# Modulation folds moved out of the key/value stage, and tile-wise hand-over of banks, in a one-core diffusion step

## The chip, the cores and the metric

The kernel runs on one NeuronCore of a Trainium2 chip. Its engines are TensorE (PE: matmuls; PEld: its weight loads), VectorE (DVE), ScalarE (ACT), GpSimd (POOL) and SyncE (SP), which issues most DMAs; each runs its own instructions in order and waits for the others through semaphores. The metric is the device time of one execution in microseconds, the median of several runs. Lnnn is a line of the kernel before; in the changed kernel the same statement has a number that is two or three higher.

## The reference

One layer of a hybrid diffusion backbone over 1024 latent tokens and 128 context tokens (1152 in all, 9 tiles of 128), model width 1024, float32:

```
m  = silu(c) @ w_ada + b_ada            # six vectors per condition ("modulation")
h  = rmsnorm(x) * (1 + scale) + shift
[u | q | k | v | gates] = h @ w_in      # 512 | 1024 | 256 | 256 | 2048 columns
f  = real(fft2(u))                      # 4 groups of 128 channels
a  = windowed attention(q, rope(k), v)  # 16 heads, 4 kv heads of 64, window 128, sink logit
x1 = x + g1 * (merge(f @ w_fo, a @ w_ao, sigmoid(gates)) @ w_out)
y  = x1 + g2 * (relu(h2 @ w1)**2 @ w2)  # h2: x1 normed and modulated
```

Latent queries read a window of latent keys and 128 cached context keys in one softmax; context queries read context keys alone. Keys and values of the context are outputs too. The modulation is computed for two condition vectors. The attention, norms and the rest of the modulation need only parts of m at a time.

## The kernel before

**Precision and weights.** A float32 matrix is split into a high part and a remainder ("whi" and "wlo", by `split`: an ACT cast at L144, a DVE subtraction at L139), and a product takes three matmuls (L192 to L194, L230 to L232). Weights come as "wraw" by SP's queue (L153).

**Stages in the profiled execution.** 0 to 174 us: norm, Fourier projection, gates, DFT. 174 to 302 us, the KV stage: `tok_proj_round` projects keys and values for the token tiles in ROUNDS, 6 tiles in round 0 and 3 in round 1, eight blocks k of the contraction each; between the rounds stand the six query pieces of head group 0. Each tile has one PSUM bank "x" of pool qk, which `evac_kv` empties (values: L691; keys: rope on DVE, or L708 for the context tile; the context outputs go through "ra" and "rb" at L711). 302 to 747 us, attention. Then the Fourier branch's output, the gate and attention-output stage from 800 us, and the output projection and MLP.

**Attention.** 36 units, one for each head group g and query block i. A unit has four score heads (`score_head`: two matmuls L755 and L756 into "s", a masked minimum on DVE L757, exp on ACT L767, and after each pair of heads the scaling on POOL L779), then for every key block a transpose group `out_t` (L789 into "ptp", the cast "ph" L792 on ACT and the remainder "pl" on DVE) and a value product `out_v` (L804 and L805 into the single bank "o"; after the last one the copy "ot" L813 and the addition "at" L814 empty it). Keys are transposed by `put_k` (L835, cast "kth" L837). TensorE's order in the KV stage and in attention is written out by hand (`manual_schedule`); the other engines' orders come from a scheduler. `unit_order` lists a unit's steps with None at each spot where fill may go: the fill steps are query pieces of the next group, gate pieces and parts of the Fourier output (L926, L947). `NSPR` sets how many are spread over the units; the rest stays for the end. The value product of block 0 stands right behind the third out_t of its own unit; the others stand between the score heads of the next unit (`late`).

**Modulation.** The remaining four vectors are computed in 16 blocks of 256 columns by ten steps each (`mod_blocks`). Steps 0 to 7 load a piece "mraw" of w_ada (L303), multiply it by a number per partition for two conditions on ACT (L307, into "macc" in step 0, into the one "mprod" buffer after that), and add on POOL (L309). In later stages both are one DVE operation (L316). Steps 8 and 9 transpose and reduce on DVE (L325, L326) into "red". `mod_fold` sums over partitions with a matmul of 16 columns (L272), and DVE adds the bias into "mods". A fold is issued at step 5 of the next block. Before each k of a KV round some steps are issued (50 in the two rounds), in attention one after each pair of heads (60 in all), ten behind attention, and 40 later. Two gate vectors are written to the scratch tensor ga_d and read back broadcast (L1106).

**Pools.** A tile pool that reuses the memory of an earlier, closed pool starts, without further words, only when all work on the earlier one is done. With reuse_waits="tile" each tile waits for the users of its own piece alone.

## Time and profile before

| | us |
|---|---|
| median of 3 runs (lowest, highest) | 1721.02 (1719.16, 1723.3) |
| the profiled execution's own time | 1719.39 |
| its span | 1717.6 |
| TensorE busy | 1621.3 |
| DVE, ACT, POOL busy | 1133.9, 909.4, 279.1 |
| KV stage to the first key transpose | 174.4 to 302.6 |
| attention | 302.6 to 747 |

The span is what the trace covers; the own time is 1.8 us longer. A row of a timeline gives start, duration, engine and line, the operation with output <- inputs, its shape, and in brackets how long the engine had stood idle before and who released it. Matmuls are pipelined: the distance of two starts, not the duration, is what one costs. The row of a window gives its length, then each engine's busy time and instructions, TensorE's granted clock (1.00 is full), the DMA engines' busy share and GB/s.

### The profile page before, as it was taken

The page shows a single profiled execution, that of the slowest core. Times are in us where ns is not written, and L with a number is a line of the kernel's source. Part 1 is how long each engine was busy: PE and PEld are TensorE (multiplying, and loading weights), DVE is VectorE, ACT ScalarE, POOL GpSimd, SP SyncE. Part 2 cuts the span into 40 slices and gives each one's busy share as a digit, 9 for nine tenths or more (in the row PEclk, how much of TensorE's full clock was granted, in tenths as well). Part 3 has the DMA queues.
Part 4 walks back from the last instruction along what each step waited for, and adds up shares of the span by engine and source line. Part 5 has one row for each costly group of instructions (what it writes and reads, how often), then busy time and mean ns, then how long its engine had stood idle before and what let it go on. Part 6 is the DMA issues. An engine that isn't in the chain of part 4 may idle for free.

```text
span 1717.6 us, 24946 instructions
## 1 busy us (share of the span) xinstructions
PE 1621.3 (94%) x8421; PEld 1426.9 (83%) x8421; DVE 1133.9 (66%) x2164; ACT 909.4 (53%) x1759; POOL 279.1 (16%) x375
## 2 busy tenths in 40 slices
PE   6999396999999999999999989999999999999998
PEld 5799385898998989979988788888888888888887
DVE  6563056576676776777557877777775588777764
ACT  7733344567577666646336574444444354444542
POOL 1010353334344443310001400000000200000000
PEclk9999698999999999999999999999999999999999
DMA  8441356943445342269545425445446896656751
GB/s 296 132 142 68 118 159 167 187 131 101 108 126 152 100 117 74 87 205 299 173 171 194 166 99 174 154 163 168 162 160 156 264 392 230 190 186 196 243 173 62
DMA packets 221136, 285.41 MB, mean 166 GB/s; under 512 B 30968, under 2 KB 148664, under 8 KB 220880
## 3 DMA queue, kind: packets, MB, share of 16 engines
q1 hardware_dynamic: 212752, 273.85, 50.4%
q0 software_dynamic: 8256, 9.96, 2.5%
q8 instruction: 66, 1.08, 0.3%
q14 instruction: 62, 0.51, 0.1%
HBM read 205.87 MB, written 77.88 MB: 165 GB/s over the span
## 4 chain that ended last, share of the span: by engine, by line
PE 70%; DVE 5%; DMA 3%; ACT 3%; issue 2%; POOL 1%; SPq 1%; DVEq 0%; ACTq 0%; POOLq 0%
PE x L1845 6%; PE x L1843 6%; PE x L1844 6%; PE x L1447 6%; PE x L1449 6%; PE x L1448 6%; PE mm L192 4%; PE mm L194 4%; PE mm L193 4%; PE ptp L789 2%; PE x L194 2%; PE x L193 2%; PE x L192 2%; PE s L756 2%; PE o L805 2%
## 5 line engine op out<-in xcount | busy, mean ns | idle before, releaser
L139 DVE TENSOR_TENSOR wlo<-wraw,whi 128x1024 fp32r<-128x1024 f32 x109 | 139.9, 1285 | 99.4 <-ACT whi L144 98.8
L144 ACT CAST whi<-wraw 128x1024 fp32r<-128x1024 f32 x107 | 111.8, 1049 | 88.2 <-DMA wraw<-in_w_in_dram 22.5
L193 PE MATMUL mm<-BR,whi 128*128 128x384 f32 x408 | 137.9, 338 | 0.0
L767 ACT ACTIVATE pt<-pt,mx 128x513 f32<-128x513 f32 (+2 forms) x144 | 95.9, 666 | 75.6 <-DVE mx L757 72.4
L1844 PE MATMUL x<-BR 128*128 128x512 f32 (+1 forms) x348 | 132.8, 382 | 0.0
L192 PE MATMUL mm<-BR,whi 128*128 128x384 f32 x360 | 129.4, 360 | 3.0 <-DVE qt L633 2.1
L1845 PE MATMUL x<-BR 128*128 128x512 f32 (+1 forms) x348 | 132.2, 382 | 0.0
L1843 PE MATMUL x<-BR 128*128 128x512 f32 (+1 forms) x348 | 131.3, 382 | 0.0
L779 POOL TENSOR_SCALAR pt<-pt,mx 128x512 f32<-128x512 f32 (+2 forms) x144 | 95.9, 679 | 212.9 <-DVE mx L777 212.6
L757 DVE CUSTOM_DVE_ANT_0 pt<-s,mask,nsink 128x512 f32<-128x512 f32 (+2 forms) x144 | 96.4, 671 | 41.4 <-PE s L756 40.2
L194 PE MATMUL mm<-BR,wlo 128*128 128x384 f32 x360 | 122.3, 340 | 0.0
L309 POOL TENSOR_TENSOR macc<-macc,mprod 128x512 f32<-128x512 f32 x77 | 102.1, 1326 | 42.9 <-ACT mprod L307 32.8
L139 DVE TENSOR_TENSOR pl<-ptp,ph 128x512 fp32r<-128x512 f32 x124 | 82.9, 686 | 38.2 <-ACT ph L792 37.6
L1816 ACT CAST BR<-aa 128x512 fp32r<-128x512 f32 x80 | 49.7, 621 | 101.7 <-PE x L1844 46.3
L307 ACT ACTIVATE mprod<-mraw,siluc 128x256 f32<-128x256 f32 x154 | 70.2, 502 | 46.8 <-POOL macc L309 45.8
L1447 PE MATMUL x<-BR,whi 128*128 128x512 f32 (+2 forms) x204 | 79.4, 389 | 4.1 <-ACT ZR L1471 2.8
L193 PEld LDWEIGHTS mm<-BR,whi 128*128 128x128 f32 x408 | 77.9, 191 | 6.3
L792 ACT CAST ph<-ptp 128x512 fp32r<-128x512 f32 x124 | 69.9, 583 | 20.3 <-PE ptp L789 18.7
L1449 PE MATMUL x<-BR,wlo 128*128 128x512 f32 (+2 forms) x204 | 77.9, 382 | 0.0
L1448 PE MATMUL x<-BR,whi 128*128 128x512 f32 (+2 forms) x204 | 77.6, 380 | 0.0
L192 PE MATMUL mm<-BT,whi 128*128 128x384 f32 x216 | 76.5, 354 | 0.0
L1844 PEld LDWEIGHTS x<-BR 128*128 128x128 f32 x348 | 65.4, 188 | 12.9
(450 smaller groups left out, 4733.6 us busy)
## 6 DMA issues: line engine op xcount, KB each, us to landing
aa<-hr_d SPq DMA_DIRECT2D x108, 256.0 KB
ab<-in_w_ff_dram SPq DMA_DIRECT2D x108, 256.0 KB
hr_d<-ZR SPq DMA_DIRECT2D x104, 256.0 KB
wraw<-in_w_in_dram SPq DMA_DIRECT2D x41, 512.0 KB
wraw<-in_w_ff_dram SPq DMA_DIRECT2D x34, 512.0 KB
mraw<-in_w_ada_dram SPq DMA_DIRECT2D x96, 128.0 KB
wraw<-in_w_out_dram SPq DMA_DIRECT2D x24, 512.0 KB
z_d<-z SPq DMA_DIRECT2D x48, 192.0 KB
```

Of the source, the lines that this page charges most:

```text
L139: eng.tensor_tensor(dst, raw, hi.bitcast(F32), ALU.subtract)
L144: nc.scalar.copy(hi, raw)
L192: nc.tensor.matmul(out, ah, bh, start=start, stop=False)
L193: nc.tensor.matmul(out, ah, bl, start=False, stop=False)
L194: return nc.tensor.matmul(out, al, bh, start=False, stop=stop).ins
L309: nc.gpsimd.tensor_tensor(acc, acc, pr_, ALU.add)
L1447: nc.tensor.matmul(po, wh, xh, start=(k == 0 and not cont), stop=False, skip_group_check=cont)
L1448: nc.tensor.matmul(po, wh, xl, start=False, stop=False, skip_group_check=cont)
L1449: nc.tensor.matmul(po, wl, xh, start=False, stop=(k == 3), skip_group_check=cont)
L1843: nc.tensor.matmul(ps, xh, bh, start=start, stop=False, skip_group_check=cont)
L1844: nc.tensor.matmul(ps, xh, bl, start=False, stop=False, skip_group_check=cont)
L1845: nc.tensor.matmul(ps, xl, bh, start=False, stop=stop, skip_group_check=cont)
```

## The change

- **Folds.** From the KV rounds to the end of attention no fold is issued at step 5. Instead, after each unit from the fourth on, one block is folded, as long as one younger one is there. "red" has 8 buffers in place of 2.
- **Modulation steps.** 30 before the KV rounds' blocks k (round 0 alone: 4 each, 2 before the last), none in round 1; in attention from the second unit on, two steps after the first pair of heads and one after the second, until 60 are left (70 steps over 24 units); 20 behind attention, and 40 later as before.
- **Hand-over.** Pools pq, q1 and q3 wait by tile. The two query buffers "qT" lie in two pools, pq and p1.
- **Value products.** All of a unit's products stand between the score heads of the next unit; ph and pl have 4 buffers in place of 3.
- **Tail.** 11 fill steps in place of 6 are kept for the end, one after each of the last value products.
- **Other.** Two "fo" buffers in place of one; dynamic_dma_scratch_size=4096, by which more SBUF is free and the small pool pk (rope, ra, qr) lies in memory of its own, so that SP's queue has the loads of rope and of the cached keys and values among the first ones.

```diff
-MOD_A = (1, 1)
+MOD_A = (2, 1)
-MOD_B = 50
+MOD_B = 60
...
-    def mod_fold():
+    fold_auto = [True]
+
+    def mod_fold(keep=0, most=99):
         nb = MB // P
-        while fold:
+        for _ in range(min(most, len(fold) - keep)):
             blk, red = fold.pop(0)
...
-                    if k == 5:
+                    if k == 5 and fold_auto[0]:
                         mod_fold()
...
-                        st["r"] = const.tile([P, 2, MB // 32], F32, tag="red", name=nm("red"), bufs=2)
+                        st["r"] = const.tile([P, 2, MB // 32], F32, tag="red", name=nm("red"), bufs=8)
...
-            tok_proj_round(ROUNDS[0], OFF_KV, bankk, evac_kv, before=lambda k: mod_step(4))
+            fold_auto[0] = False
+            tok_proj_round(ROUNDS[0], OFF_KV, bankk, evac_kv, before=lambda k: mod_step(4 if k < 7 else 2))
             for piece in q_pieces(0):
...
-            tok_proj_round(ROUNDS[1], OFF_KV, bankk, evac_kv, before=lambda k: mod_step(2 if k < 7 else 4))
-        pq = s1x.enter_context(tc.tile_pool(name="pq", bufs=1))
-        q1 = s1x.enter_context(tc.tile_pool(name="q1", bufs=1, space=PSUM))
+            tok_proj_round(ROUNDS[1], OFF_KV, bankk, evac_kv)
+        pq = s1x.enter_context(tc.tile_pool(name="pq", bufs=1, reuse_waits="tile"))
+        q1 = s1x.enter_context(tc.tile_pool(name="q1", bufs=1, space=PSUM, reuse_waits="tile"))
...
-            qt = pq.tile([P, 4, CH], F32R, tag="qT", name=nm("qT"), bufs=2)
+            qt = (pq if (g * NJ + j) % 2 else p1).tile([P, 4, CH], F32R, tag="qT", name=nm("qT"), bufs=1)
...
-            if len(msteps) > MOD_B:
+            if len(msteps) > MOD_B and u["s"]:
                 with tc.issue_after(ins.ins):
                     mod_step(min(MOD_A[pr], len(msteps) - MOD_B))
...
-            ph = p1.tile([P, 512], F32R, tag="ph", name=nm("ph"), bufs=3)
-            pl = p1.tile([P, 512], F32R, tag="pl", name=nm("pl"), bufs=3)
+            ph = p1.tile([P, 512], F32R, tag="ph", name=nm("ph"), bufs=4)
+            pl = p1.tile([P, 512], F32R, tag="pl", name=nm("pl"), bufs=4)
...
             for b in range(nb):
                 out += [lambda b=b: out_t(prev, b), None]
-                if b == 2:
-                    out += [None, lambda: out_v(prev, 0), None]
-            if 0 < nb < 3:
-                out += [None, lambda: out_v(prev, 0), None]
-            late += [(prev, b) for b in range(1, nb)]
+            late += [(prev, b) for b in range(nb)]
             return out
...
-        NSPR = NSUB - 16 - 6
+        NSPR = NSUB - 16 - 11
...
             pending = u
+            if s > 2:
+                mod_fold(1, 1)
+        out_t(pending, 0)
         for v in late:
+            fill_to(base + 1)
             out_v(*v)
-            fill_to(base + 1)
-        out_t(pending, 0)
+            base += 1
         fill_to(NSUB)
...
         man.close()
+        fold_auto[0] = True
         mod_step(len(msteps) - MOD_B)
         mod_fold()
 
-    q3 = ctx.enter_context(tc.tile_pool(name="q3", bufs=6, space=PSUM))
+    q3 = ctx.enter_context(tc.tile_pool(name="q3", bufs=6, space=PSUM, reuse_waits="tile"))
...
-            return y, p3.tile([P, D], F32, tag="fo", name=nm("fo"), bufs=1)
+            return y, p3.tile([P, D], F32, tag="fo", name=nm("fo"), bufs=2)
...
-    nc = _bacc.Bacc("TRN2", target_bir_lowering=False, num_devices=1)
+    nc = _bacc.Bacc("TRN2", target_bir_lowering=False, num_devices=1, dynamic_dma_scratch_size=4096)
```

How the change moves instructions, at three places.

TensorE in round 0 of the KV stage, where the first block's fold stood (waits shown in brackets; x is a token tile's bank). Before:

```order
L231 MATMUL x_1723<-wlo_1700,BR 128x512
L232 MATMUL x_1723<-whi_1699,BR 128x512
L272 MATMUL mm_1745<-red_1679,quads 128x16 [waits DVE_49]
L230 MATMUL x_1703<-whi_1699,BR 128x512
L231 MATMUL x_1703<-wlo_1700,BR 128x512
```

and now:

```order
L231 MATMUL x_1723<-wlo_1700,BR 128x512
L232 MATMUL x_1723<-whi_1699,BR 128x512
L230 MATMUL x_1703<-whi_1699,BR 128x512
L231 MATMUL x_1703<-wlo_1700,BR 128x512
L232 MATMUL x_1703<-whi_1699,BR 128x512
```

The fold has left the round; the first one now stands in attention behind the fourth unit.

TensorE at the boundary from the KV stage to attention. Before:

```order
L232 MATMUL x_2335<-whi_2465,BT 128x512
L835 MATMUL ptp_2540<-ident,kd_1619 128x128 [waits DMAHW3_49,DMAHW2_49,DMAHW4_49,DMAHW1_49,DMAHW5_49,DMAHW0_49,DMAHW6_49,DVE_49,DMAHW7_49,Activation_49,Pool_49]
L835 MATMUL ptp_2540<-ident,kd_1619 128x128 [waits Pool_49]
L835 MATMUL ptp_2540<-ident,kd_1619 128x128
L835 MATMUL ptp_2540<-ident,kd_1619 128x128 [waits Pool_49]
L192 MATMUL mm_2559<-BR,whi_2549 128x384
```

and now:

```order
L232 MATMUL x_2270<-whi_2333,BT 128x512
L838 MATMUL ptp_2408<-ident,kd_1619 128x128 [waits DMAHW3_49,DMAHW4_49,DMAHW2_49,DMAHW5_49,DMAHW1_49,DMAHW6_49,DMAHW0_49,DMAHW7_49,PE_49,Pool_49]
L838 MATMUL ptp_2408<-ident,kd_1619 128x128 [waits Pool_49]
L838 MATMUL ptp_2408<-ident,kd_1619 128x128
L838 MATMUL ptp_2408<-ident,kd_1619 128x128 [waits Pool_49]
L192 MATMUL mm_2427<-BR,whi_2417 128x384 [waits Activation_49]
```

The first key transpose no longer waits for DVE and ACT, which empty the last tiles' banks; it waits for DMAs, for TensorE's own earlier work and for the keys' copy on POOL. The first query matmul behind it waits for a weight cast on ACT.

ACT in the KV stage: weight casts among the modulation's multiplications. Before:

```order
L307 ACTIVATE macc_1686<-mraw_1687,siluc 128x256 x2
L307 ACTIVATE mprod_1729<-mraw_1727,siluc 128x256 x2
L307 ACTIVATE mprod_1735<-mraw_1733,siluc 128x256 x2
L307 ACTIVATE mprod_1741<-mraw_1739,siluc 128x256 x2
L144 CAST whi_1951<-wraw_1949 128x1024
L307 ACTIVATE mprod_1753<-mraw_1751,siluc 128x256 x2
```

and now:

```order
L480 COPY z_1595<-mm_1570 128x384
L144 CAST whi_1928<-wraw_1926 128x1024
L309 ACTIVATE macc_1632<-mraw_1633,siluc 128x256 x2
L309 ACTIVATE mprod_1639<-mraw_1637,siluc 128x256 x2
L309 ACTIVATE mprod_1645<-mraw_1643,siluc 128x256 x2
L309 ACTIVATE mprod_1651<-mraw_1649,siluc 128x256 x2
L144 CAST whi_2042<-wraw_2040 128x1024
```

The cast of round 0's last pair of weights (whi_1951 before, whi_1928 now) stood behind the first block and part of the second; now it stands ahead of the whole chain, and the cast of the first query weights (whi_2042) comes within its first five steps.

More of the change, by code (lines that the diff above doesn't have):

```diff
@@ L1035, in begin @@
                     qts[g1, i1 // 3] = load_qt(g1, i1 // 3)
-            return {"g": g, "i": i, "q": qts[g, i // 3], "v": kv[g][1], "pts": [], "p": {}}
+            return {"s": s, "g": g, "i": i, "q": qts[g, i // 3], "v": kv[g][1], "pts": [], "p": {}}
         def next_keys(g, i):
```

## The prediction

> **What bounds the kernel now.** I read the page's totals and 40 slices first, then TensorE's waits, then the stretch in which they lie by its timeline and windows, and last ACT, POOL and the DMA queue around it.
>
> ```profile
> span 1717.6 us, 24946 instructions
> PE 1621.3 (94%) x8421; PEld 1426.9 (83%) x8421; DVE 1133.9 (66%) x2164; ACT 909.4 (53%) x1759; POOL 279.1 (16%) x375
> ...
> PEclk9999698999999999999999999999999999999999
> ```
>
> TensorE's waits (us in total, times, longest):
>
> ```profile
> PE mm L272 <- DVE red L326: 30.1, 2, 26.8
> PE ptp L835 <- ACT rb L711: 16.4, 1, 16.4
> ...
> PE o L804 <- DVE at L814: 9.2, 6, 2.3
> ...
> PE o L805 <- DVE pl L139: 1.4, 5, 0.6
> ```
>
> TensorE is busy for 94% of the span, so whatever shortens the kernel without removing matmuls must come out of its 96 us of gaps. The four waits are the largest gaps that this change touches: 57.1 us. The clock's slices 4 and 6, counted from 0 in steps of 43 us, sink to 6 and 8 tenths: that is where TensorE stood still. The timeline of TensorE through that stretch, 174 to 315 us:
>
> ```profile
> 174.41 0.39 PE L230 MATMUL x<-whi,BR 128*128 128x512 f32 x1
> ...
> 178.30 0.39 PE L232 MATMUL x<-whi,BR 128*128 128x512 f32 x1
> ...
> 205.54 0.61 PE L272 MATMUL mm<-red,quads 128*128 128x16 f32 x2 [26.85 <-DVE red L326]
> ...
> 206.56 0.63 PE L231 MATMUL x<-wlo,BR 128*128 128x512 f32 x1
> 206.99 0.63 PE L232 MATMUL x<-whi,BR 128*128 128x512 f32 x1
> ...
> 213.01 0.40 PE L230 MATMUL x<-whi,BR 128*128 128x512 f32 x1
> ...
> 220.04 0.39 PE L231 MATMUL x<-wlo,BR 128*128 128x512 f32 x1
> ...
> 224.63 0.37 PE L272 MATMUL mm<-red,quads 128*128 128x16 f32 x2 [3.29 <-DVE red L326]
> ...
> 242.92 0.33 PE L192 MATMUL mm<-BR,whi 128*128 128x384 f32 x1
> ...
> 269.34 0.47 PE L230 MATMUL x<-whi,BR 128*128 128x512 f32 x1
> ...
> 302.58 0.66 PE L835 MATMUL ptp<-ident,kd 128*128 128x128 f32 x2 [16.38 <-ACT rb L711]
> ...
> 315.32 0.41 PE L755 MATMUL s<-kth,qT 128*128 128x384 f32 x1 [0.99 <-ACT z L659]
> ```
>
> A window of it (length; busy us and count of PE, PEld, DVE, ACT, POOL; granted clock; DMA share; GB/s):
>
> ```profile
> 205.00:212.00 7.00, 6.46 (x16) 5.21 (x17) 1.08 (x6) 2.72 (x6) 3.73 (x3) 0.50 0.23 65
> ```
>
> TensorE does 4.3 us of round 0 and then stands for 26.85 us before a matmul of 16 columns, because the program put the first block's fold in the middle of the round. The second fold costs 3.29 us. Behind the last projection it stands 16.38 us for ACT's copy of an output tile (L711). After a stop the matmuls start 0.43 us apart (206.56 to 206.99) in place of 0.227 (213.01 to 220.04, 31 rows apart, 7.03 / 31), and the window of 205 to 212 has a granted clock of 0.50. Why the first fold is late stands in POOL's and ACT's rows:
>
> ```profile
> 186.45 0.91 ACT L307 ACTIVATE macc<-mraw,siluc 128x256 f32<-128x256 f32 x2 [10.59 <-DMA mraw<-in_w_ada_dram]
> 188.23 1.26 POOL L309 TENSOR_TENSOR macc<-macc,mprod 128x512 f32<-128x512 f32 x1 [1.09 <-ACT mprod L307]
> ...
> 190.57 1.26 POOL L309 TENSOR_TENSOR macc<-macc,mprod 128x512 f32<-128x512 f32 x1 [1.08 <-ACT mprod L307]
> ...
> 203.58 0.45 DVE L325 STREAM_TRANSPOSE mtr<-macc 128x256 f32<-128x256 f32 x1 [17.06 <-POOL macc L309]
> ```
>
> ACT multiplies, POOL adds, each waits for the other through the one mprod buffer: 190.57 - 188.23 = 2.34 us a step, eight steps a block, started by a DMA that lands at 186.
>
> **The change, part by part.** *Folds leave the KV stretch, and the banks are handed over by tile.* From 174.41 to 315.32 are 140.9 us now. The same matmuls without gaps: 216 of 512 columns at 0.227 = 49.0; the six query pieces 242.92 to 269.34 = 26.4; the two groups of key transposes (four each, 0.66 us the pair at the slow clock, so about 0.35 a group at full clock) 0.7; 48 matmuls of 384 columns at 0.17 (313.12 to 313.99 is five of them)
>
> ```profile
> 313.12 0.33 PE L192 MATMUL mm<-BT,whi 128*128 128x384 f32 x1
> ...
> 313.99 0.34 PE L194 MATMUL mm<-BT,wlo 128*128 128x384 f32 x1
> ```
>
> = 8.3. The sum is 84.4, so **-56.5**: 47.5 us are the four waits (26.85 + 3.29 + 16.38 + 0.99), the other 9.0 are the folds and the half-speed stretches behind the stops. The Trainium skill (TensorE: Matmul & The Clock Gate, Part 1: The HAM clock gate) has the clock at half after an idle window and full again after about 3.4 us of sustained work; by that the three restarts cost an estimated 3 x 1.7 = 5 us and the term would be -52.5, the time 1668.5. The rows decide against it in size: the clock is at half for all 7 us of the 205 to 212 window.
>
> What is late next in this stretch? The chain now has 30 steps, 24 of them multiplications: 186.45 + 24 x 2.34 = 243, with TensorE at round 1 from 174.4 + 32.7 + 26.4 = 233.5. Round 0's last weights are cast ahead of the chain now. Of round 1's, the second pair stands on ACT behind 18 multiplications, 186.45 + 18 x 2.34 = 229, and is needed a pair (18 matmuls, 4.1 us) after 233.5; the fourth behind 22, at 238, and is needed at 246: 8 us early. Round 0's evacuation is interleaved with the chain, its consumers 26 us away behind the query pieces. The new first wait is for weights from the DMA queue, which TensorE now reaches 40 us sooner; two casts show what that can be:
>
> ```profile
> 289.52 1.04 ACT L144 CAST whi<-wraw 128x1024 fp32r<-128x1024 f32 x1 [7.57 <-DMA wraw<-in_w_in_dram]
> ...
> 297.14 1.04 ACT L144 CAST whi<-wraw 128x1024 fp32r<-128x1024 f32 x1 [3.77 <-DMA wraw<-in_w_in_dram]
> ```
>
> The key casts (L837) are queued behind these on ACT, and the first scores wait for them. Bounds 0 and 11.3 (both in full). Both casts fall while the ga_d stores slow the DMA, and those move away, so I take **+3**.
>
> *All four value products between the next unit's scores.* The third out_t no longer pushes the first product against the one "o" bank, whose last reader is the at addition (L814): 9.2 + 1.4 us in eleven waits, of which the tail has about 1.6 (below). The bank's deadline moves back by one transpose group and one fill, by my estimate some 2 us of a unit of 12 (432 us of the stage below by 36 units), against a longest wait of 2.3. Bounds -9 and -4; **-7**. The fourth ph/pl buffer covers the longer life of the pair.
>
> *Denser modulation.* In 24 units there are three steps in place of two:
>
> ```profile
> 315.00:747.00 432.00, 418.62 (x2433) 388.52 (x2434) 303.58 (x728) 289.59 (x671) 173.96 (x274) 1.00 0.42 116
> ACT mprod L307 <- POOL macc L309: 9.2, 12, 1.6
> ACT ph L792 <- PE ptp L789: 18.7, 28, 1.8
> POOL pt L751 <- PE ptp L789: 24.8, 18, 5.8
> ```
>
> (the last three for 315 to 745). A step is 0.91 us of ACT and 1.26 of POOL. Of the 432 us ACT is free for 142, 4.0 a unit, and POOL for 258. The hand-off sits between exp (L767) and the transposes' casts; the chain already stops ACT for 9.2 us over 60 steps. Bounds 0 and 24 x 0.91 = 22 (all of ACT's extra work in TensorE's way); nearest is the row in which ACT itself waits for TensorE, with time to spare, so **+3**. The folds in this stage are as many as before, 16 columns each, and read reds that were finished a block earlier, so they wait for nothing: 0; with a red still open one would cost the second fold's 3.29.
>
> *The ga_d stores,* which need folded values, move into attention with the folds. Around 284 to 288 they leave TensorE 2.2 busy of 4 us with the DMA at 0.45:
>
> ```profile
> 284.00:288.00 4.00, 2.20 (x10) 1.50 (x8) 0.32 (x1) 0.00 (x0) 0.00 (x0) 1.00 0.45 12
> ```
>
> 12 GB/s in that window against 116 in attention: for some 10 us almost nothing else lands. The next qT or weights have about a unit of lead. Bounds 0 and 8; **+1.5**.
>
> *The tail.* Eleven fill pieces rather than six between the last products, which now wait 0.97 and 0.60 us:
>
> ```profile
> 739.29 0.47 PE L804 MATMUL o<-ph,vg 128*128 128x512 f32 x1 [0.97 <-DVE at L814]
> ...
> 741.71 0.50 PE L805 MATMUL o<-pl,vg 128*128 128x512 f32 x1 [0.60 <-DVE pl L139]
> ```
>
> Bounds -3 and 0; **-2**.
>
> *Ten more steps in the gate stage,* on DVE: 8 of 10 are two operations of 0.48 us,
>
> ```profile
> L316 DVE SCALAR_TENSOR_TENSOR macc<-mraw,siluc,macc x14: 473/479/484, 758.6 to 783.8; 128x256 f32<-128x256 f32 x14
> 800.00:900.00 100.00, 100.00 (x546) 95.86 (x546) 56.29 (x101) 41.06 (x72) 0.00 (x0) 1.00 0.59 193
> ```
>
> 7.7 us beside a TensorE that is 100% busy and a DVE at 56%. Without that cover it would be the 7.7; **+0.5**.
>
> *Loads of rope and cache ahead in SP's queue* (0.75 MB, since the smaller DMA scratch frees SBUF that they no longer share). The first 20 us move 342 GB/s:
>
> ```profile
> 0.00:20.00 20.00, 7.53 (x41) 6.97 (x42) 11.63 (x41) 15.51 (x29) 3.41 (x9) 1.00 0.89 342
> ```
>
> so 2.2 us if they stand before something TensorE waits for. Bounds 0 and 2.5; **+1**.
>
> Sum: -56.5 + 3 - 7 + 3 + 1.5 - 2 + 0.5 + 1 = **-56.5**. The profiled execution's own time is 1719.39; 1719.4 - 56.5 = 1662.9. The median of the runs is 1.6 above that execution, so I predict **1664.5 us**.
>
> **The rivals.** *R1: the boundary wait comes back as a wait for weights.* TensorE reaches the attention 56 us sooner and the casts of 289.52 and 297.14 do not come sooner by as much. For it: DMA share is 0.45 even now at 284 to 288. Against: the ga_d stores and 20 steps' loads leave the queue. All 11.3 instead of 3: 1664.5 + 8.3 = **1673**.
>
> *R2: the third step shows.* ACT's 0.91 us lands each time before a ph cast that TensorE needs: 22 instead of 3, **1683**. Against it: today the cast waits for TensorE (18.7 us), not the reverse.
>
> *R3, slower than before.* mprod has one buffer, and ACT works in order: with two steps after each first pair, ACT stands at the second multiplication until POOL has added, and POOL's add stands behind the scaling (L779) of the pair. Then exp and ph of the next heads wait through both hand-offs. Two of them at 2.34 us in 24 units are 112 us, in place of 3: **1774**. It decides from 57 / 24 = 2.4 us a unit. Against: ACT's waits for POOL here are 9.2 us in all, 1.6 at most, and a unit has 4 us of free ACT.
>
> *R4: POOL is held by the vg loads.* The smaller scratch holds fewer prepared DMA pieces. Now POOL is through one in 1.02 us while it lands after 8.1:
>
> ```profile
> L828 POOL DMA_DIRECT2D vg<-vh_d x4: 966/1020/1169, 305.5 to 535.8; - x4
> DMA to landing us min/median/max: 5.4/8.1/14.8
> ```
>
> If POOL had to stay until they land, pt scaling stands behind it: 4 x 7.1 = 28, **1693**. No row shows POOL held at such an instruction, and none shows a smaller scratch. The Trainium skill (DMA: Bandwidth & Descriptors, SWDGE vs HWDGE vs iDMA) puts the descriptors of POOL's DMAs into rings in SBUF, and what a ring does when it is too small no run here shows.
>
> *R5: the hand-over by tile doesn't act at the boundary,* because the first transpose still meets a bank of the last tile: 16.4 come back, **1681**. Against: the changed order has no wait for ACT or DVE there.
>
> **How the numbers follow.** Forecast 0.66, R1 0.12, R2 0.12, R4 0.04, R3 0.03, R5 0.03. All bounds at their good ends give 1719.4 - 56.5 - 9 - 3 + 1.6 = 1652.5; the likeliest's own range is 1652 to 1675, its far end R1 with the tail at 0. For 8 in 10 I add R2 and R5 above, and below the 2 us by which the three runs shown lie about their median: **1650 to 1684**. 0.2% (3.4 us) is what a measurement here can tell. Only R3 is slower: slower 0.03, same 0.02 (a milder R3), faster 0.95.
>
> **What would show it.** In the changed profile: no wait at the fold's matmul, TensorE from the first KV matmul to the first score in 84 to 95 us, granted clock near 1 in slices 4 to 6, no 16 us before the key transposes; waits at the first product under 4 us in attention; ACT's wait for POOL under 20 us. Wrong would be: weight waits over 11 us at the boundary (R1), TensorE's idle in attention up by over 10 us with ACT ahead of it (R2, R3), POOL's DMA instruction above 5 us (R4).

## The result, and the profile after

The changed kernel takes 1675.62 us (median of 4 runs, 1673.11 to 1677.22), the kernel before 1722.16: ratio 0.9728, 95% interval 0.9704 to 0.9752, so 46.5 us less. 1664.5 was forecast, with a range of 1650 to 1684: the direction and the range hold, and the gain is 10 us smaller than the forecast 56.5.

The page of the changed kernel's profiled execution (1677.22 us, the slowest of its four; the quoted parts are span, busy time and granted clock by slice), and its waits of TensorE:

```profile
span 1675.4 us, 24835 instructions
...
PE 1618.5 (97%) x8421; PEld 1423.5 (85%) x8421; DVE 1146.0 (68%) x2180; ACT 902.7 (54%) x1743; POOL 271.4 (16%) x368
...
PEclk9999999999999999999999999999999999999999
```

```profile
PE o L807 <- DVE at L817: 6.1, 5, 4.4
PE mm L192 <- DVE qt L635: 3.8, 2, 3.1
PE x L192 <- ACT ER L1158: 3.2, 2, 2.1
PE ptp L792 <- DVE pl L139: 3.2, 3, 1.9
...
PE s L758 <- ACT kth L840: 1.3, 1, 1.3
```

No fold and no output copy is among the waits any more; the clock's two sunken slices are gone. What is left are small waits in the place of three large ones. The first rows of three stages in the timeline, the changed kernel's ahead:

```profile
177.92 0.39 PE L230 MATMUL x<-whi,BR 128*128 128x512 f32 x1
...
257.29 0.60 PE L838 MATMUL ptp<-ident,kd 128*128 128x128 f32 x4
...
267.98 0.45 PE L758 MATMUL s<-kth,qT 128*128 128x384 f32 x1 [1.31 <-ACT kth L840]
...
833.69 0.48 PE L1281 MATMUL x<-whi,BR 128*128 128x512 f32 x1
```

```profile
875.87 0.47 PE L1278 MATMUL x<-whi,BR 128*128 128x512 f32 x1
```

The last is the kernel before, where the output projection begins. With the rows of the prediction this gives the account of the two profiled executions:

| stage | before | changed | difference | forecast |
|---|---|---|---|---|
| to the KV stage's first matmul | 174.4 | 177.9 | +3.5 | +1 |
| KV stage to the first score | 140.9 | 90.1 | -50.8 | -53.5 |
| first score to the output projection | 560.6 | 565.7 | +5.2 | -4 |
| the rest of the span | 841.7 | 841.7 | 0 | 0 |
| sum | 1717.6 | 1675.4 | -42.2 | -56.5 |

The KV stage gave nearly what was forecast. The front took 2.5 us more than its term, and the third row is 9 us off and on the wrong side. One execution of each kernel stands behind the table. The medians differ by 46.5, which leaves about +1 for the third row if the first two hold, and a kernel below that has the same attention took 560.5 us for it. So up to 5 us of this row is the spread of single executions. The experiments go to these two rows, and to how the large term divides.

### The profile page after: what moved, and what is told of

The parts are those of the page before. It is cut to its first block, busy times and chain, and to the rows that moved or that the text cites. A ratio compares the mean times of both kernels' runs of the same rounds, so it can differ in the third digit from the quotient of the medians.

```text
span 1675.4 us, 24835 instructions
## 1 busy us (share of the span) xinstructions
PE 1618.5 (97%) x8421; PEld 1423.5 (85%) x8421; DVE 1146.0 (68%) x2180; ACT 902.7 (54%) x1743; POOL 271.4 (16%) x368
## 4 chain that ended last, share of the span: by engine, by line
PE 72%; DVE 5%; DMA 3%; issue 2%; ACT 2%; POOL 1%; SPq 1%; DVEq 0%; ACTq 0%; POOLq 0%
PE x L1848 6%; PE x L1847 6%; PE x L1846 6%; PE x L1450 6%; PE x L1451 6%; PE x L1452 6%; PE mm L192 4%; PE mm L194 4%; PE mm L193 4%; PE ptp L792 2%; PE x L194 2%; PE x L192 2%; PE x L193 2%; PE s L758 2%; PE s L759 2%
## 5 line engine op out<-in xcount | busy, mean ns | idle before, releaser
L192 PE MATMUL mm<-BR,whi 128*128 128x384 f32 x360 | 129.1, 359 | 4.6 <-DVE qt L635 3.8
L311 POOL TENSOR_TENSOR macc<-macc,mprod 128x512 f32<-128x512 f32 x70 | 93.5, 1335 | 40.4 <-ACT mprod L309 32.8
L193 PEld LDWEIGHTS mm<-BR,whi 128*128 128x128 f32 x408 | 77.3, 190 | 6.3
L309 ACT ACTIVATE mprod<-mraw,siluc 128x256 f32<-128x256 f32 x140 | 63.8, 504 | 31.6 <-POOL macc L311 27.3
L139 DVE TENSOR_TENSOR BR<-aa,BR 128x512 fp32r<-128x512 f32 x80 | 55.0, 687 | 34.8 <-ACT BR L1819 34.3
L192 PEld LDWEIGHTS mm<-BR,whi 128*128 128x128 f32 x360 | 68.0, 189 | 11.8 <-DVE qt L635 4.4
L792 PE MATMUL ptp<-ident,pt 128*128 128x128 f32 x496 | 74.0, 273 | 3.2 <-DVE pl L139 3.2
```

The source lines that it names most:

```text
L139: eng.tensor_tensor(dst, raw, hi.bitcast(F32), ALU.subtract)
L192: nc.tensor.matmul(out, ah, bh, start=start, stop=False)
L193: nc.tensor.matmul(out, ah, bl, start=False, stop=False)
L792: nc.tensor.transpose(pst[:, h * P : (h + 1) * P], u["pts"][h // 2][:, h % 2, b * P : (b + 1) * P], ident)
```

## Experiments

Each median was taken beside runs of the kernel before on the same chip (1720.2 to 1722.3 us). Every kernel here computes the whole output. Stage lengths in the text are differences of the first rows of two stages in that kernel's timeline, as in the table above.

### Which part of the KV stage's gain is whose

**Folds alone, on the kernel before.** The edit to the kernel before, with two others that make room and keep the first stage as it was (dynamic_dma_scratch_size=4096, loads of rope and cache behind the DFT's):

```diff
-                    if k == 5:
+                    if k == 5 and fold_auto[0]:
                         mod_fold()
...
+            fold_auto[0] = False
             tok_proj_round(ROUNDS[0], OFF_KV, bankk, evac_kv, before=lambda k: mod_step(4))
...
             pending = u
+            if s > 2:
+                mod_fold(1, 1)
```

> The kernel before with the folds alone taken out of the KV stage (8 red buffers, one fold after each unit from the fourth on; the smaller scratch, without which the red buffers don't fit, and the loads of rope and cache queued where they were). The 50 modulation steps of the KV stage stay. Prediction's view: the two fold waits and their slow stretches go, 26.85 + 3.29 + about 6 = 36, the boundary wait of 16.4 stays: 1684 to 1688. Rival: the chain of 50 steps (40 multiplications of 2.34 us from 186 on, to about 280) still ends when it did, and TensorE, 36 us earlier at the boundary, waits for ACT there until the last tiles are emptied: the boundary wait grows to 30 us or more and the time is 1695 to 1710. Then the smaller number of steps before attention is as much a part of the gain as the folds are.

Measured: 1685.42 us, ratio 0.9803 (0.9772 to 0.9834): 36.3 us less, as the prediction's view had it. Its waits of TensorE from 170 to 290 us:

```profile
PE ptp L841 <- ACT rb L714: 8.7, 1, 8.7
PE mm L192 <- DVE qt L635: 4.1, 2, 3.3
PE s L761 <- DMA qT<-q_d: 3.3, 1, 3.3
```

The fold's waits are gone, and the boundary's has not grown but halved (16.4 to 8.7) though all 50 steps are still there. The likely reading, not tested alone, is that part of the old 16.4 us belonged to the ga_d stores, which go to attention with the folds: ACT, which copies the last tile, stood 7.57 and 3.77 us for weight loads before, and stands 1.47 us for one here.

**Hand-over by tile alone, on the kernel before.**

```diff
-        pq = s1x.enter_context(tc.tile_pool(name="pq", bufs=1))
-        q1 = s1x.enter_context(tc.tile_pool(name="q1", bufs=1, space=PSUM))
+        pq = s1x.enter_context(tc.tile_pool(name="pq", bufs=1, reuse_waits="tile"))
+        q1 = s1x.enter_context(tc.tile_pool(name="q1", bufs=1, space=PSUM, reuse_waits="tile"))
```

(and pool q3 likewise).

> The kernel before with the hand-over by tile of pools pq, q1 and q3 alone. Prediction's view: the 16.38 us at the boundary go and 1 to 3 us of slow clock behind them: 1702 to 1705. Rival: the weight casts of 289.52 and 297.14, which waited 7.57 and 3.77 us for their loads behind the ga_d stores, come no earlier, so the query matmuls and the first scores wait for them: 1709 to 1721.

Measured: 1719.18 us, ratio 0.9987 (0.9972 to 1.0001): no difference that can be told. TensorE's and SP's timelines around the boundary:

```profile
296.62 1.09 PE L835 MATMUL ptp<-ident,kd 128*128 128x128 f32 x4 [3.82 <-DVE rb L686]
312.27 0.66 PE L755 MATMUL s<-kth,qT 128*128 128x384 f32 x1 [11.36 <-DMA qT<-q_d]
```

```profile
281.67 0.52 SPq L1106 DMA_DIRECT2D ga_d<-mods  x1
...
283.60 10.16 SPq L303 DMA_DIRECT2D mraw<-in_w_ada_dram  x2
...
303.99 4.17 SPq L736 DMA_DIRECT2D qT<-q_d  x8
```

What SP itself waited for in this stretch:

```profile
SPq L303 <- DMA mraw<-in_w_ada_dram: 8.3, 1, 8.3
...
SPq L736 <- DMA out_k_dram<-ra: 0.8, 1, 0.8
```

The rival was right in kind, wrong in its object. The 16.38 us wait becomes 3.82, and 11.36 us come back 16 us later: not weights are late but the query tiles qT. The row of 10.16 us covers two modulation loads, and 8.3 us of it are SP's wait, right after the ga_d stores, for an earlier such load to land. The loads of qT come later still: they stand on SP behind the context outputs (L712) and then wait for the store of "ra" to land. So they are as late as the emptying of the last tiles, whatever becomes of the banks. In the changed kernel the first query tile lies in pool p1, and its loads are issued 38 us ahead of the first score:

```profile
229.83 2.11 SPq L739 DMA_DIRECT2D qT<-q_d  x4
```

That second pool is part of the change's hand-over and is not in this run; the hand-over of the banks alone bought nothing. The kernel with the two, without the folds' move, was not run.

**The changed kernel without that hand-over in pq and q1** (the same two lines, undone).

> The changed kernel without the hand-over by tile in pools pq and q1. If its worth is that of the wait it took away, 16 us are lost: 1690 to 1695. If the earlier end of the chain (30 steps in place of 50) alone has the last tiles emptied sooner, the boundary wait is 5 to 9 us: 1680 to 1686.

Measured: 1683.32 us, ratio 0.9784 (0.976 to 0.9808), 7.7 us more than the changed kernel, in the range of the second expectation. One wait has come back:

```profile
PE ptp L838 <- ACT rb L713: 8.4, 1, 8.4
```

With all 50 steps it was 8.7 us (folds alone), so the smaller number of steps is not what halved it. The division is: folds (with the stores they move) 36.3, hand-over in pq and q1 7.7 once they are gone and nothing before that, some 2.5 for the rest. The prediction had booked 16.4 to the hand-over. From the first score to the output projection this kernel, whose attention is that of the changed one, takes 560.5 us in place of 565.7.

### The passage through attention

**ga_d stores later.** `att_st` collects the attention output's stores:

```diff
-    ga_rows(2, 0)
+    with tc.issue_after(att_st[55].ins):
+        ga_rows(2, 0)
     ga_put(0)
```

> The changed kernel with one edit: the two ga_d stores are queued on SP behind the attention store of the 28th unit, where the DMA engines are least busy, in place of the 8th. TensorE's own order is unchanged. Theory: in the changed kernel the stores (362 us) hold up SP (one modulation load takes 6.99 us to issue) and all DMA; ACT waits 3.35 us for that load and TensorE 4.42 us at 382 with a granted clock of 0.93 over the 46 us around it, so 4.4 + 3 are lost there. Expected 1668 to 1670 us, no wait over 1.5 us before a first value product. Rival, the denser modulation steps: the stall is theirs, the stores only happened to lie near; then another load is late and the time stays at 1674 to 1677.

Measured: 1672.11 us, ratio 0.9714 (0.9696 to 0.9732). First the stall in the changed kernel, by SP, ACT and TensorE and the window around it, then the same window with the stores moved:

```profile
362.40 1.00 SPq L1109 DMA_DIRECT2D ga_d<-mods  x2
...
367.78 6.99 SPq L305 DMA_DIRECT2D mraw<-in_w_ada_dram  x2
```

```profile
378.85 0.91 ACT L309 ACTIVATE mprod<-mraw,siluc 128x256 f32<-128x256 f32 x2 [3.35 <-DMA mraw<-in_w_ada_dram]
```

```profile
382.43 0.77 PE L807 MATMUL o<-ph,vg 128*128 128x512 f32 x1 [4.42 <-DVE at L817]
```

```profile
362.00:408.00 46.00, 41.58 (x229) 38.38 (x229) 27.66 (x76) 31.23 (x77) 23.70 (x34) 0.93 0.70 130
```

```profile
362.00:408.00 46.00, 43.57 (x257) 40.41 (x256) 31.78 (x85) 34.18 (x83) 23.63 (x34) 1.00 0.54 134
```

SP's row of 6.99 us covers two modulation loads. The first is issued in 1.76 us; before the second, SP waits, by the profile for a ga_d store to land:

```profile
SPq L305 <- DMA ga_d<-mods: 4.8, 1, 4.8
```

ACT, in order, waits 3.35 us for the load that came late, ahead of ph, exp and the output copies, and TensorE at the end of that row 4.42 us. With the stores 250 us later a stop of 2.43 us remains at this place, the clock stays at 1.00, and TensorE has 28 more matmuls done in these 46 us. The 16 score heads around the stop (33rd to 49th) take 44.5 to 45.8 us in the five kernels that have it, and 41.2 to 42.3 in the four with the stores moved (three of them with the first product back in its own unit): 3.1 us apart in the mean. From the first score to the output projection it is 559.8 us in place of 565.7, but 560.5 in the kernel without the hand-over, with the same stop (4.45 us) in it, so that difference is not the stores' price. By medians the 3.5 us lie inside the two intervals together; the stretch of score heads is what shows this term. The store writes a column of 4-byte numbers. The Trainium skill (DMA: Bandwidth & Descriptors, Rules for kernel authors) says that a last dimension that is not contiguous makes a descriptor of each element, and advises rearranging. What it would be with rows no run here shows.

**Steps spread thinner.**

```diff
-MOD_A = (2, 1)
+MOD_A = (1, 1)
```

> The changed kernel with one modulation step after each pair of heads (two a unit over 35 units) in place of two and one (three a unit over 24). If the denser steps cost time (the rival: ACT and POOL hand off too often for the unit), it is 4 to 20 us faster, 1656 to 1671. If ACT's 4 us of free time a unit cover the third step, as the prediction had it with +3, it is 1672 to 1677, with ACT's waits for POOL about as they are (6.9 us).

Measured: 1680.9 us, ratio 0.976 (0.9742 to 0.9778): 5.3 us more, which neither side expected. The wait that came:

```profile
687.02 0.90 PE L950 MATMUL mm<-BR,whi 128*128 128x130 f32 x3 [7.73 <-ACT macc L935]
```

The Fourier pieces among the last fill steps use the buffer "macc" (L935) for their partial result. With 35 units of steps a block is still open when they begin, and the piece waits until DVE has emptied it. The third step a unit is also the means to be through by unit 24. What it costs is left open: the clock is at 0.50 from 684.4 to 694.6 us, and without the 7.73 us and half of the 7.58 us of TensorE's work in that stretch the row from the first score to the output projection would be some 556 us by my estimate (567.6 measured), below the 560.5 to 565.7 with the third step.

**More steps in attention.**

```diff
-MOD_B = 60
+MOD_B = 50
```

> The changed kernel with 80 modulation steps in attention (to unit 27) in place of 70, so that 10 and not 20 are left for the passage to the gate stage, as before the change. Theory: that passage is bound by the DMA engines (0.97 of their time, 308 GB/s, from 722 to 757 us), and eight more loads of 128 KB there are 1 MB or 3.4 us, which show as TensorE's waits for ACT's ER casts (1.2 us before the change, 3.2 with it): 1672 to 1673.5, those waits at 1 us or less, no new stall in attention. Rival, the prediction's view: the ten steps are covered by a TensorE that is 100% busy, the waits stay, and the time is 1674 to 1677.

Measured: 1680.13 us, ratio 0.9766 (0.9752 to 0.9779): 4.5 us more. My theory falls: eight loads fewer behind attention left TensorE's wait for the ER casts at 3.8 us, and new waits came before the first value products. Where the 4.5 us went is not shown: from the first score to the last product the profiled executions take 437.7 us here and 439.0 in the changed kernel, and from there to the output projection 129.5 and 126.8. Its waits from 550 to 836 us:

```profile
PE x L192 <- ACT ER L1158: 3.8, 1, 3.8
PE o L807 <- DVE at L817: 3.6, 3, 2.8
```

**First value product back in its own unit.**

```diff
             for b in range(nb):
                 out += [lambda b=b: out_t(prev, b), None]
+                if b == 2:
+                    out += [None, lambda: out_v(prev, 0), None]
+            if 0 < nb < 3:
+                out += [None, lambda: out_v(prev, 0), None]
-            late += [(prev, b) for b in range(nb)]
+            late += [(prev, b) for b in range(1, nb)]
```

> The changed kernel with the value product of block 0 back behind the third transpose group of its own unit; the tail and all else as changed. If the prediction's term (-7) is right, TensorE's waits before the first product come back to about 9 us in all and the time is 1680 to 1684. Rival: the move is worth little, because the bank was then late for another reason (ACT behind a late load), and the time stays within 2 us of 1675.6.

Measured: 1673.39 us, ratio 0.9719 (0.97 to 0.9738), so the move is worth nothing or less than nothing, near the rival's range. Its waits in attention:

```profile
PE o L808 <- DVE pl L139: 4.3, 6, 2.0
PE o L807 <- ACT ph L795: 4.2, 4, 1.6
PE o L807 <- DVE at L817: 2.2, 3, 1.7
```

10.7 us of waits at the products, as many as before the change, but another kind: for the cast and the remainder, not for the bank. In the changed kernel the products wait for 7.2 us (6.1 and 1.1), of which 4.4 is the stall above; in their place stand waits of the next transposes for DVE (3.2), of a score (1.0) and of a Fourier piece (1.4). With the product in its own unit that stall is gone though the stores stand at the same place (the longest wait from 340 to 410 us is 1.6), so the stall seems to take both, a late load and a product that comes soon after it.

**The tail as it was.**

```diff
-        NSPR = NSUB - 16 - 11
+        NSPR = NSUB - 16 - 6
...
-        out_t(pending, 0)
         for v in late:
-            fill_to(base + 1)
             out_v(*v)
-            base += 1
+            fill_to(base + 1)
+        out_t(pending, 0)
```

> The changed kernel with the tail as it was: 6 fill steps kept for the end in place of 11, the last transposes behind the last products. The prediction has the new tail at -2, so without it 1677 to 1679. Rival: in the profile the new tail is no gain, since from the 112th score head to the gate stage's first matmuls of the output projection the changed kernel takes 237.7 us and the kernel before 230.5: then 1672 to 1676.

Measured: 1674.83 us, ratio 0.9746 (0.9732 to 0.976): the same within the intervals. In the trace it reaches the output projection 3.9 us sooner after the first score (561.8 against 565.7), but it also has a longer wait for the ER casts, 4.8 us.

### The first stage

**Rope and cache loads where they were.** `dft_ld` is the last load of the DFT's matrices; the loads of the cached values and keys get the same line:

```diff
-            nc.sync.dma_start(rope, rope_in)
+            with tc.issue_after(dft_ld.ins):
+                nc.sync.dma_start(rope, rope_in)
```

> The changed kernel with the loads of rope and of the cached keys and values queued on SP behind the DFT's loads, near where they stood in the kernel before; TensorE's order in the first stage is then that of the kernel before. Theory: these 0.75 MB ahead of the modulation's first weights make the first stage 3.5 us longer (34.0 to 34.7 us for the first projection matmul, then 2.4 and 3.5). Expected: the KV stage starts at 174.4 in place of 177.9, and 1672 us. Rival: the 3.5 us are the spread of one execution to the next; then the start moves by less than 1 us and the time is 1674 to 1677.

Measured: 1670.22 us, ratio 0.9701 (0.9683 to 0.972), and the KV stage starts at

```profile
174.96 0.39 PE L230 MATMUL x<-whi,BR 128*128 128x512 f32 x1
```

Windows of 20 to 30 and 30 to 40 us, the changed kernel's ahead:

```profile
20.00:30.00 10.00, 10.00 (x70) 7.18 (x68) 8.89 (x18) 6.78 (x12) 1.62 (x1) 1.00 1.01 351
30.00:40.00 10.00, 8.08 (x36) 6.91 (x37) 8.13 (x10) 9.28 (x13) 0.00 (x0) 0.83 0.72 244
```

```profile
20.00:30.00 10.00, 10.00 (x72) 7.37 (x70) 9.58 (x18) 7.23 (x12) 1.62 (x1) 1.00 0.83 270
30.00:40.00 10.00, 8.87 (x41) 7.18 (x40) 8.18 (x10) 8.61 (x12) 0.00 (x0) 0.83 0.83 265
```

With the loads early the DMA engines are full at 20 to 30 us, and TensorE loses its matmuls (36 in place of 41) ten microseconds later. In the profiled executions of all kernels here the KV stage starts at 177.3 to 179.1 us with the loads early (seven kernels) and at 173.8 to 177.6 with them late (five): 3.0 us apart in the mean, 178.4 against 175.4, with a spread of 3.7 among the five. Of the 5.4 us by medians that leaves 2.4, of which the profile has 1.7 in the KV stage (88.3 us in place of 90.1); why is not shown.

### Together

**Three edits: e_rope, e_ga and e_outv.**

> The changed kernel with three edits together: rope and cache loads behind the DFT's loads, ga_d stores behind the 28th unit, the first value product back behind the third transpose group. Alone they gave -5.4, -3.5 and -2.2 us against the changed kernel's 1675.6. If they add, 1663 to 1667; if the three medians were partly spread, and the attention's waits replace one another, 1667 to 1671.

Measured: 1670.71 us, ratio 0.9706 (0.9679 to 0.9734). They do not add to 1664.5. In the profiled execution the KV stage starts at 177.6, not 175.0; the product's place shows no gain once the stores have moved (first score to output projection 560.6, against 559.8 with the stores moved alone); and TensorE's wait for the ER casts behind attention, 3.2 us in the changed kernel, has grown:

```profile
PE x L192 <- ACT ER L1167: 6.0, 1, 6.0
```

**All edits, with more buffers for the query pieces.** The changed kernel waits in the KV stage for DVE (L635), which itself waits for the store of the pair before (L634, "qt" has one buffer). To the three edits come MOD_B = 50, ph and pl with three buffers, the stores behind the 29th unit, and

```diff
-                t[n] = p1.tile([P, CH], F32, tag=f"qt{n}", name=nm("qt"), bufs=1)
+                t[n] = p1.tile([P, CH], F32, tag=f"qt{n}", name=nm("qt"), bufs=2 if n < 2 else 1)
```

> The changed kernel with all edits that paid: rope and cache loads behind the DFT's, ga_d stores behind the 29th unit, the first value product back behind the third transpose group with three ph/pl buffers, 10 steps left behind attention, and, in the memory so freed, two buffers for the first two rope products of a query piece, for which TensorE waited 3.1 to 3.2 us (the store of the pair before had not landed). If each wait is its own: 1670.7 (the three edits together) - 3 (query pieces) - 3 (passage) = 1663 to 1666. Rival: what is saved ahead of the passage is given back in it, because the DMA engines set its end (TensorE's wait for the first ER cast was 6.0 us in the kernel with three edits, 3.2 in the changed one): 1668 to 1671.

Measured: 1668.3 us, ratio 0.9701 (0.9688 to 0.9715), in the rival's range but not by its mechanism: TensorE's wait for the ER casts is 3.5 us in place of 6.0. The KV stage takes 85.8 us as hoped, and 437.8 in place of 429.1 us pass from the first score to the last product.

**The same with MOD_B = 60 again** and the stores behind the 28th unit.

> The changed kernel with three edits (rope and cache loads behind the DFT's loads, ga_d stores behind the 28th unit, the first value product back behind the third transpose group) and two buffers for the first two rope products of a query piece, in the memory of the fourth ph/pl buffers; 70 steps in attention as in the changed kernel. It differs from the kernel with three edits (1670.7) by the buffers alone, and from the one with all edits (1668.3) by the 70 steps in place of 80. Theory: the buffers take 4 us out of the KV stage (90.0 to 85.8 in the profile of the kernel with all edits) and the 80 steps cost 2 to 4 in attention: 1664 to 1667. Rival: the saving is given back in attention, with about 560 us from the first score to the output projection in both: 1668 to 1671.

Measured: 1666.22 us, ratio 0.9678 (0.966 to 0.9696); the interval lies wholly below the changed kernel's (0.9704 to 0.9752), and the time is in the theory's range. Its KV stage, and what is left of the query pieces' wait:

```profile
174.30:259.90 85.60, 84.22 (x418) 74.36 (x416) 51.62 (x82) 41.76 (x84) 31.27 (x35) 1.00 0.67 207
```

```profile
PE mm L192 <- DVE qt L635: 0.5, 1, 0.5
```

85.6 us against the 84.4 that the prediction counted for a stage without gaps. This is the best version: 54.3 us under the kernel before, 9.4 under the changed one by the medians.

## Why the prediction was right, and where it was off

**The range held with some luck.** The median lies 11.1 us above the forecast, just beyond the likeliest's own range (to 1675, its far end R1), in the part that was added for R2 and R5. None of these came. The 11 us come from other terms, nearly all missed on the same side, and two of them beyond their own bounds: the value products (-9 to -4) and the loads (0 to 2.5).

**The large term was right in sum, wrong in its parts.** -56.5 was worked out as the stage without gaps. The stage has 90.1 us with one unforeseen wait and 85.6 without it. But the four waits were booked as if each ended by its own edit. The folds took 36.3 of them, the hand-over 7.7; alone the hand-over took none, because the query tiles, which TensorE needed next, came as late as the emptying of the last tiles. That the change gives the first query tile memory of its own seems to be part of this gain (with folds alone, where it has none, qT still cost 3.3 us), and the prediction has no term for it.

**New waits in the KV stage: +3 forecast, 5.7 found** (90.1 - 84.4). The size is near, the object was wrong. Not weights from the DMA queue (R1), but the query pieces' own store: 3.1 of the 3.8 us at L635 are one stop for DVE, whose tile still had to land in memory. That row stood in the trace of before as a wait of 1.0 us (L192 on "qt") and I had passed over it; a TensorE that is no longer held back runs into the next shortest buffer.

**Value products: -7 forecast, about 0 found, the step that failed.** I counted the waits at the products and took them as removable. They are the end of a chain through ACT and DVE, both in order; moving the product moved the wait to other instructions (transposes, scores), and putting it back brought other waits for the same 10.7 us. The sign set for it failed too: waits at the first product were to stay under 4 us and are 6.1, of which 4.4 are the one stall behind the ga_d stores.

**Denser steps: +3 forecast, not measured alone.** R3's 112 us and R2's 22 did not come: ACT's waits for POOL are 7.9 us in the changed kernel's attention (9.2 before), and the whole row is 5.2 us longer in the profile. Spreading the steps thinner made it 5.3 us slower, but through a stop of its own, so a price of some us for the third step is not excluded. What the prediction did not see is the other end: the steps must be through before the Fourier pieces need "macc".

**ga_d: +1.5 forecast, about 3 found** (3.1 by the score heads, 3.5 by medians), within its bounds of 0 and 8. The mechanism was named, the cover was not there: "a unit of lead" holds for qT, not for the modulation's own load on which ACT stands in order.

**The tail (-2) and the ten steps in the gate stage (+0.5)**: undoing the tail changed nothing that the medians can tell, so its gain is not seen; taking the ten steps out of the passage did not shorten TensorE's wait for ER, so their cover holds. What the prediction missed is that the passage itself is bound by something else: from the first load of the attention's output to the last ER cast it is 35.4 us before, 35.0 in the changed kernel and 34.3 to 37.3 in the others. The two windows below are this passage in the changed kernel and in the kernel before:

```profile
711.00:746.00 35.00, 31.79 (x187) 29.00 (x187) 26.96 (x54) 16.75 (x39) 0.00 (x0) 1.00 0.91 283
```

```profile
750.00:786.00 36.00, 34.83 (x192) 31.22 (x193) 24.97 (x49) 17.10 (x39) 0.00 (x0) 0.95 0.83 255
```

The DMA engines are busy for 0.91 and 0.83 of it, and it is no shorter where they are less busy, so full DMA engines alone do not set its length. TensorE, which reaches its first ER matmul 22.3 us after the last value product in place of 26.2, waits there (1.2 us before, 3.2 in the changed kernel, up to 6.0). Fewer modulation loads did not shorten it; what sets it stays open.

**Loads of rope and cache: +1 forecast, 3.5 found** (3.0 in the mean of the kernels above). The row of 342 GB/s gave 2.2 us for the bytes. What the rest is stays open: the clock at 30 to 40 us is 0.83 in place of 1.00 before, but it is so in three of the five kernels with the loads late too. Those three start the KV stage at 175.0 to 177.6 us, the two at 1.00 at 173.8 and 174.3, so the clock has a part in the spread.

**R4 and R5.** POOL is through a vg load in 1.0 us as before, with the smaller scratch:

```profile
L831 POOL DMA_DIRECT2D vg<-vh_d x4: 963/1024/1167, 270.1 to 493.7; - x4
```

and the key transposes follow the last projection at once (257.06 + 0.23 to 257.29), so the hand-over acts.

## What to carry to other kernels

A wait of 16 us with a clean name can be a place where two late things meet: take one away and the other stands there, so a term for a wait that is removed holds only if what comes next on the same engine is known to be ready. Small background work that shares a buffer with later work must be through before that work begins, and transfers of single numbers belong where nothing stands behind them in the queue. Where the next stage waits for its own loads, some of what is saved ahead of it can be given back as a wait inside it. And single executions of the same code differed by 5 us over 560 here, so a term of a few us is better read from one short stretch in several kernels than from one long row.

## What the runs showed of the chip

Whether the granted clock falls after a stop of TensorE is not decided by the length of that stop alone. After 3.11 us in the changed kernel the matmuls of 384 columns start 0.18 us apart at once:

```profile
232.47 0.45 PE L192 MATMUL mm<-BR,whi 128*128 128x384 f32 x1 [3.11 <-DVE qt L635]
232.75 0.34 PE L193 MATMUL mm<-BR,whi 128*128 128x384 f32 x1
232.93 0.35 PE L194 MATMUL mm<-BR,wlo 128*128 128x384 f32 x1
```

After 2.15 us in the kernel before they start 0.32 us apart:

```profile
426.66 0.48 PE L804 MATMUL o<-ph,vg 128*128 128x512 f32 x1 [2.15 <-DVE at L814]
...
427.31 0.52 PE L192 MATMUL mm<-BR,whi 128*128 128x384 f32 x1
427.63 0.52 PE L193 MATMUL mm<-BR,whi 128*128 128x384 f32 x1
```

The Trainium skill (TensorE: Matmul & The Clock Gate, Part 1: The HAM clock gate) has the clock fall after an idle window of about 3.4 us. As a limit for a single stop the traces do not bear that out: 2.15 us were enough, and 3.11 us were not.

How long the slow clock lasts can differ between two executions for nearly the same stop. After the stop of 4.42 us in the changed kernel the clock is at 0.50 for 6.83 us, of which 5.6 us are work (from 382.43 on):

```profile
381.23:388.06 6.83, 5.63 (x16) 5.08 (x17) 3.32 (x9) 4.52 (x12) 3.35 (x4) 0.50 1.08 232
388.10:391.50 3.40, 3.40 (x22) 3.28 (x21) 1.69 (x6) 2.25 (x7) 2.21 (x3) 1.00 0.65 178
```

In the kernel without the hand-over in pq and q1 the stop is 4.45 us, and the clock is back after 3.4 us of work (from 393.15 on):

```profile
393.15:396.53 3.38, 3.38 (x10) 3.09 (x11) 1.00 (x2) 2.69 (x7) 2.85 (x4) 0.50 0.99 232
396.60:400.00 3.40, 3.40 (x20) 3.19 (x19) 2.55 (x7) 2.01 (x5) 0.85 (x2) 1.00 1.35 263
```

The same section of the Trainium skill has the clock rise after about 3.4 us of sustained work. The second execution agrees; the first took longer.

The stop of 2.43 us with the stores moved left the clock at 1.00, and the 16 score heads around it take 41.2 us, against 45.8 in the changed kernel: in these two executions 4.6 us for a stop that is 2.0 us shorter.
